# Sums of weight blocks made ahead on VectorE and kept in DRAM, and a first tile split on VectorE with first rows from ScalarE's queue

## The chip, the core and the metric

The kernel runs on one core of a Trainium2 chip. Its engines are TensorE (PE in the profile, its weight loads PEld), VectorE (DVE), ScalarE (ACT), GpSimd (POOL) and SyncE (SP). SyncE here only issues transfers; ScalarE and GpSimd issue a few as well. Each engine works through its own instructions in order and waits for others by semaphores. The metric is the device time of one execution in microseconds (us), lower is better. What a profile calls the span is the time from the first to the last instruction that it records.

## The reference

One encoder layer: a sandwich of RMSNorms around a gated neighbourhood attention, with 512 tokens (a grid of 8 x 64), width 2048, and 16 heads of 128, all in float32.

```python
h = rms_norm(x, norm_pre[i])
o, z = na_mixer(h, na_w_in[j], na_rpb[j])   # q, k, v, z = split(h @ w_in, 4); attention over 8 x 16 neighbours with a bias
y = (o * jax.nn.silu(z)) @ w_out
x = x + rms_norm(y, norm_post[i])
```

Nearly all of the work is the two products `h @ w_in` (512 x 2048 by 2048 x 8192) and `(...) @ w_out` (512 x 2048 by 2048 x 2048).

## The kernel before

**Numbers.** A float32 value is split into a high part `hi` (rounded to the matmul's fp32r form, a cast) and a low part `lo` (the value minus `hi`, a subtraction on VectorE). A product is then three matmuls: hi by hi, hi by lo, lo by hi. So each 128 x 512 block of weights W costs one cast (L247, ScalarE) and one subtraction (L248, VectorE) before it can be used. This is `prep(m)`; `m` counts the slots of the whole program, and `prep` runs two slots ahead (`AHEAD`) of the matmuls. Three `hi`/`lo` buffers go round.

**Steps.** The products are made in ten steps. Steps 0 and 8 are plain: 32 slots of 12 matmuls each. Steps 1 to 7 (the steady steps) and step 9 (`LAST`) use Strassen-Winograd: the four blocks B11, B12, B21, B22 of W are combined into seven operands, and seven passes of 8 slots with 6 matmuls each take the place of eight. Step 9 takes the passes in the order of `LATE`, 0, 1, 3, 4, 6, 5, 2. The sums of W that a pass needs are made in eight tiles `T[k]`, one for each block of rows k: pass 0 uses B11, pass 1 adds B12, pass 3 adds B22, pass 4 adds B21; pass 6 is B12 + B22 in the last step. Each addition is one VectorE instruction (L240) with a second operand `raw`, loaded from W into one of four buffers (`NRAW`). A raw load is issued by SP when its buffer is free and at least six preparations ahead. The other passes use one block alone, as `raw`.

**Beside the matmuls.** The attention of the heads (transposes, scores, exponentials, normalization) is laid between the slots by a table, `HEAD`, with calls `at(slot, function)`. In the last step the results are finished: `finish` squares and scales, `final` scales with the row's factor, adds x and writes out. The combining operations of the seven passes (`combine`, L359 to L380) are additions on VectorE that read the accumulators.

**Order.** Each engine's instructions are laid out by a scheduler that starts from the program's order and moves what is ready; what goes through `sync`, `dve` and `act` (the class `InOrder`) keeps its place in program order. Gated outputs of the heads are kept in DRAM by GpSimd's queue (`keep_g`, the tensor `graw`) and fetched for step 8.

**The start.** SP loads x0, raw0, x1, raw1, x2, raw2, x3 in turn, the first at 0.74 us and then one each 0.46 us or so. ScalarE issues the load of `gcol`, loads its activation table, multiplies x0 by `gcol` (`take_x`, L158), casts its two halves (`split_a`, L147) and then casts raw0 (L247). Transfers of one queue reuse eight semaphores, so a transfer can wait for the one eight places before it.

## Time and profile before

| what | us |
|---|---|
| median of 3 runs | 895.92 (895.0 to 896.43) |
| the profiled execution | 896.13 |
| its span | 894.4 |
| first plain matmul starts | 5.97 |
| steady steps, step 1 to step 7 | about 92 to 706 |
| last step's first matmul | 802.74 |
| last matmul starts | 883.83 |
| last instruction on VectorE ends | 890.1 |

The page gives, for each engine, its busy time; a table of windows gives the same for stretches of time. "Releaser" or "waits" name what an idle engine waited for. In a group of instructions `t<-t,raw` means: the tile t written from t and raw; buffer numbers are left out.

### The profile page before, as it was taken

To read this page: it belongs to the slowest core of one execution; us is meant where nothing else is said; L and a number is where in the kernel's file an instruction comes from. 1 tells how busy PE (TensorE), PEld (TensorE's weight loads), DVE (VectorE), ACT (ScalarE), POOL (GpSimd) and SP (SyncE) were. 2 spreads that over 40 slices of the span, in tenths; PEclk is the share of its full clock that TensorE was granted. 3 is DMA by queue.
4 is the path that set the end of the run, shared out by engine and by line. 5 is a ranking of instruction groups with operands and counts; after the bars stand their busy time and mean duration, and the time that the engine had idled before them with its cause. 6 is when DMAs were issued, how large, how long until landed. Compare 5 with 4: busy or idle time off the path is not lost. (4 is left out here: it accounts for less than half of the span.)

```text
span 894.4 us, 13143 instructions
## 1 busy us (share of the span) xinstructions
PE 877.7 (98%) x4184; PEld 729.3 (82%) x4184; DVE 733.8 (82%) x1367; ACT 560.7 (63%) x1093; POOL 21.0 (2%) x42
## 2 busy tenths in 40 slices
PE   9999999999999999999999999999999999999995
PEld 8888888888888888888888888888888788888774
DVE  4567979897988898889878987998799845979987
ACT  7666857585758565856675667566766755555451
POOL 0000000000000000000000000000010100000000
PEclk9999999999999999999999999999999999999998
DMA  8768357646763765377547654774486534447877
GB/s 267 210 178 257 97 173 237 204 121 184 234 192 109 223 216 178 115 224 226 167 121 226 210 174 124 235 211 149 147 271 218 157 100 139 141 141 226 269 231 239
DMA packets 88277, 168.65 MB, mean 189 GB/s; under 512 B 10128, under 2 KB 10128, under 8 KB 88208
## 3 DMA queue, kind: packets, MB, share of 16 engines
q1 hardware_dynamic: 85536, 159.95, 59.4%
q0 software_dynamic: 2240, 7.34, 2.4%
q8 instruction: 32, 0.52, 0.2%
q10 hardware_dynamic: 432, 0.53, 0.2%
q14 instruction: 37, 0.30, 0.1%
HBM read 159.92 MB, written 7.86 MB: 188 GB/s over the span
## 5 line engine op out<-in xcount | busy, mean ns | idle before, releaser
L247 ACT CAST hi<-t 128x512 fp32r<-128x512 f32 x320 | 196.6, 618 | 132.2 <-DVE lo L248 21.5
L248 DVE TENSOR_TENSOR lo<-t,hi 128x512 fp32r<-128x512 f32 x320 | 217.3, 686 | 33.5 <-ACT hi L247 32.7
L248 DVE TENSOR_TENSOR lo<-raw,hi 128x512 fp32r<-128x512 f32 x184 | 125.9, 688 | 68.6 <-ACT hi L247 46.9
L247 ACT CAST hi<-raw 128x512 fp32r<-128x512 f32 x184 | 113.8, 620 | 99.2 <-PE u L285 24.7
L240 DVE TENSOR_TENSOR t<-t,raw 128x512 f32<-128x512 f32 x200 | 134.0, 686 | 7.5 <-DMA raw<-in_w 6.6
L285 PE MATMUL u<-hi,a 128*128 128x512 f32 x512 | 130.9, 392 | 1.4 <-DVE e L380 1.2
L285 PEld LDWEIGHTS u<-hi,a 128*128 128x128 f32 x512 | 94.9, 188 | 21.5 <-DVE e L380 1.8
L285 PE MATMUL u<-lo,a 128*128 128x512 f32 x256 | 70.8, 389 | 0.0
L285 PEld LDWEIGHTS u<-lo,a 128*128 128x128 f32 x256 | 48.0, 188 | 10.0
L255 DVE TENSOR_TENSOR t<-t,raw 128x512 f32<-128x512 f32 x56 | 37.3, 686 | 7.3 <-DMA raw<-in_w 7.3
L332 PE MATMUL u9Y<-hi,a 128*128 128x512 f32 x96 | 26.6, 393 | 0.5 <-ACT hi L247 0.5
L332 PE MATMUL u1Y<-hi,a 128*128 128x512 f32 x96 | 26.8, 396 | 0.0
L332 PE MATMUL u2Y<-hi,a 128*128 128x512 f32 x96 | 26.8, 396 | 0.0
L332 PE MATMUL u4Y<-hi,a 128*128 128x512 f32 x96 | 26.8, 396 | 0.0
L332 PE MATMUL u3Y<-hi,a 128*128 128x512 f32 x96 | 26.8, 396 | 0.0
L332 PE MATMUL u5Y<-hi,a 128*128 128x512 f32 x96 | 26.8, 396 | 0.0
L332 PE MATMUL u7Y<-hi,a 128*128 128x512 f32 x96 | 26.8, 396 | 0.0
L332 PE MATMUL u6Y<-hi,a 128*128 128x512 f32 x96 | 26.8, 396 | 0.0
L332 PEld LDWEIGHTS u9Y<-hi,a 128*128 128x128 f32 x96 | 17.8, 188 | 5.4 <-ACT hi L247 1.4
L545 POOL DMA_DIRECT2D graw<-zm x14 | 7.8, 554 | 561.7 <-DVE zm L539 561.7
L495 ACT ACTIVATE edge<-edge,nm 128x192 f32<-128x192 f32 x32 | 14.5, 455 | 8.7 <-DVE nm L488 8.7
L332 PEld LDWEIGHTS u4Y<-hi,a 128*128 128x128 f32 x96 | 17.4, 188 | 3.2
(446 smaller groups left out, 1924.1 us busy)
## 6 DMA issues: line engine op xcount, KB each, us to landing
raw<-in_w SPq DMA_DIRECT2D x392, 256.0 KB, 3.0
t<-in_w SPq DMA_DIRECT2D x128, 256.0 KB, 3.0
bm<-in_rpb SPq DMA_DIRECT2D x16, 384.0 KB, 3.3
x<-in_xT SPq DMA_DIRECT2D x16, 256.0 KB, 3.9
graw<-zm POOLq DMA_DIRECT2D x14, 256.0 KB, 3.4
sq<-in_x SPq DMA_DIRECT2D x6, 512.0 KB, 6.2
xres<-in_x SPq DMA_DIRECT2D x12, 256.0 KB, 4.1
out<-xres SPq DMA_DIRECT2D x10, 256.0 KB, 3.0
```

What stands on the lines that cost most here:

```text
L240: nc.vector.tensor_tensor(T[k], T[k], src, ALU.add)
L247: nc.scalar.copy(hi, src)
L248: nc.vector.tensor_tensor(lo, src, hi.bitcast(F32), ALU.subtract)
L255: nc.vector.tensor_tensor(T[k], T[k], src, ALU.add)
L285: nc.tensor.matmul(U[n][j], l, r, start=k == 0 and i == 0, stop=k == KT - 1 and i == 2)
L332: nc.tensor.matmul(U[c][s], l, r, start=p in (0, 1, 4) and k == 0 and n == 0, stop=k == KH - 1 and n == 2, skip_group_check=True,)
L495: nc.scalar.activation(p, p, AF.Exp, bias=nm[:, i : i + 1], accum_out=sm[:, i : i + 1])
L545: nc.gpsimd.dma_start(graw[h], z_of[h])
```

## The change

**Sums of W for the last step.** The four sums that step 9 needs for each k (for passes 6, 1, 3 and 4) are made ahead, in steps 0 to 7. For each k, B12 and B22 of step 9 are loaded into two tiles Z (by SP for k = 0, by GpSimd's queue for the others). Four additions on VectorE follow, with B11 and B21 as `raw` loads that take their turn in the four raw buffers. Each sum is written to a DRAM tensor `wsum` by SP. The slots are in a list: four in each steady step, at slots 3, 16, 23 and 51 of the step. The Z tiles of the next k can be loaded only when the sums in them have been written out.

In step 9 the tile `T[k]` is loaded with the finished sum of the next pass as soon as its present content has been split; the additions and their raw loads are gone, and only the last pass (2) uses raw loads.

**The start.** raw0 and raw1 are loaded by ScalarE's queue. The activation table is loaded after that. The cast of raw0 is made on VectorE. For the first four k, ScalarE's multiplication and casts keep program order.

**Small tiles.** The four row-sum columns (`rc`, `rcy`, `ms`, `msy`) are slices of one tile `rows`, those of the softmax (`mx`, `sm`, `nm`, `rs`) of one tile `col`; `ms3` is `ms`.

```diff
-    nc.scalar.preload_act_table_set("exp_and_others")
...
+    Z = [cp.tile([P, L], F32, name=f"z{i}") for i in range(2)]
+    wsum = dp.tile([NPASS, KH, P, L], F32, name="wsum")
+    LATE_W = {p: wsum[p] for p in (1, 3, 4, 6)} | {0: w[LAST, B11], 5: w[LAST, B22]}
+
+    SUMS = ((1, None, 6), (0, B11, 1), (1, B11, 3), (1, B21, 4))
+
+    def load_z(k):
+        for t, q in zip(Z, (B12, B22)):
+            (nc.gpsimd if k else nc.sync).dma_start(t, w[LAST, q, k])
+
+    def sum_z(k, i):
+        z, add, p = SUMS[i]
+        if i in (1, 3):
+            sum_z.raw = raws.pop(N + 2 * k + i // 2)
+        nc.vector.tensor_tensor(Z[z], Z[z], Z[0] if add is None else sum_z.raw, ALU.add)
+
+    def keep_z(k, i):
+        z, _, p = SUMS[i]
+        nc.sync.dma_start(wsum[p, k], Z[z])
...
     def take_x(k):
-        nc.scalar.activation(X[k], X[k], AF.Copy, scale=gcol[:, k : k + 1])
-        take(k)
+        scalar = act if k < 4 else nc.scalar
+        scalar.activation(X[k], X[k], AF.Copy, scale=gcol[:, k : k + 1])
+        take(k, scalar)
...
+    slots = [base(step) + c for step in range(1, NSTEP) for c in (3, 16, 23, 51)]
+    sums = {}
+    for k in range(KH):
+        for i in range(4):
+            sums.setdefault(slots[3 * k + k // 2 + (0, 1, 1, 2)[i]], []).append((k, i))
+    first = {k: slots[3 * k + k // 2 - 1] + 3 if k else base(1) - 8 for k in range(KH)}
...
     def load_raw(m):
         raws[m] = wp.tile([P, L], F32, tag="raw", name=f"raw{m}", bufs=NRAW)
+        if m >= N:
+            k, i = divmod(m - N, 2)
+            nc.sync.dma_start(raws[m], w[LAST, (B11, B21)[i], k])
+            return
...
-        nc.sync.dma_start(raws[m], src)
+        (nc.scalar if m < 2 else nc.sync).dma_start(raws[m], src)
...
-        if not plain and (p in (1, 3, 4) or step == LAST and p == 6):
+        if step < NSTEP and not plain and p in (1, 3, 4):
             nc.vector.tensor_tensor(T[k], T[k], src, ALU.add)
...
-        nc.scalar.copy(hi, src)
+        if m == 0:
+
+            nc.vector.tensor_copy(hi, src)
+        else:
+            (act if m < 4 else nc.scalar).copy(hi, src)
         nc.vector.tensor_tensor(lo, src, hi.bitcast(F32), ALU.subtract)
-        if plain:
+        if step == LAST:
+            i = LATE.index(p)
+            if i + 2 < NPASS:
+                nc.sync.dma_start(T[k], LATE_W[LATE[i + 1]][k])
+        elif plain:
...
+    for k in range(KH):
+        at(first[k], load_z, k)
...
+    nc.scalar.preload_act_table_set("exp_and_others")
     for m in range(-AHEAD, N):
         if m + AHEAD < N - KH:
             prep(m + AHEAD)
+            for j in z_raws(m + AHEAD):
+                for r in at_prep.get(j, ()):
+                    load_raw(r)
+            for k, i in sums.get(m + AHEAD, ()):
+                sum_z(k, i)
+                at(m + AHEAD + 1, keep_z, k, i)
```

The change in the order is shown at three places. The first is VectorE at the very start: `raw_156` and `raw_154` are the first tile of W, `a_0` and `a_1` the two halves of a block of x. Before:

```order
L148 TENSOR_TENSOR a_0_110<-x_154,a_0_110 128x256 [waits Activation_49]
L148 TENSOR_TENSOR a_1_111<-x_154,a_1_111 128x256 [waits Activation_49]
L248 TENSOR_TENSOR lo_174<-raw_156,hi_173 128x512 [waits DMAHW2_49,Activation_49]
L248 TENSOR_TENSOR lo_187<-raw_160,hi_186 128x512 [waits DMAHW4_49,Activation_49]
L148 TENSOR_TENSOR a_0_114<-x_158,a_0_114 128x256 [waits Activation_49]
```

and now:

```order
L286 CAST hi_172<-raw_154 128x512 [waits DMAHW2_49]
L289 TENSOR_TENSOR lo_173<-raw_154,hi_172 128x512 [waits DVE_49]
L169 TENSOR_TENSOR a_0_108<-x_152,a_0_108 128x256 [waits Activation_49]
L169 TENSOR_TENSOR a_1_109<-x_152,a_1_109 128x256 [waits Activation_49]
L169 TENSOR_TENSOR a_0_112<-x_156,a_0_112 128x256 [waits Activation_49]
```

The cast of the first tile now stands on VectorE and waits for its load alone; both parts of W stand ahead of the two low parts of x.

The second place is VectorE at the turn from step 3 to step 4, where the fourth row block's last sum and the fifth one's first sum stand (`z_149` and `z_148` are the two Z tiles; DMASW is GpSimd's queue). In the run of splits L248 of the profile, these rows now stand:

```order
L289 TENSOR_TENSOR lo_3691<-t_142,hi_3690 128x512 [waits Activation_49]
L141 TENSOR_TENSOR z_149<-z_149,raw_3744 128x512 [waits DMAHW5_49,DMAHW0_49,DVE_49]
L289 TENSOR_TENSOR lo_3704<-t_143,hi_3703 128x512 [waits PE_49,Activation_49]
L443 TENSOR_TENSOR vl_0_3753<-s_3_2988,vh_0_3752 128x512 [waits Activation_49]
L289 TENSOR_TENSOR lo_3718<-t_144,hi_3717 128x512 [waits DVE_49,PE_49,Activation_49]
L289 TENSOR_TENSOR lo_3729<-t_145,hi_3728 128x512 [waits PE_49,Activation_49]
L289 TENSOR_TENSOR lo_3740<-t_146,hi_3739 128x512 [waits PE_49,Activation_49]
L289 TENSOR_TENSOR lo_3759<-t_147,hi_3758 128x512 [waits PE_49,Activation_49]
L289 TENSOR_TENSOR lo_3770<-t_140,hi_3769 128x512 [waits DMAHW4_49,PE_49,Activation_49]
L141 TENSOR_TENSOR z_149<-z_149,z_148 128x512 [waits DMASW5_49,DMASW3_49]
L277 TENSOR_TENSOR t_140<-t_140,raw_3813 128x512 [waits DMAHW1_49,DVE_49]
L289 TENSOR_TENSOR lo_3780<-t_141,hi_3779 128x512 [waits DMAHW6_49,PE_49,Activation_49]
```

The scheduler has moved the first sum of the fifth block up to eight rows behind the last sum of the fourth, both in the same tile `z_149`. In between, the fourth block's sum has to be written out and the fifth block's B22 loaded. In the profile of before the first and the last but three of these rows are the splits at 344.25 and 352.00 us.

The third place is VectorE in the last step, ahead of the combining operations of pass 4 (L363 before, L408 now), which TensorE waits for before it goes on with pass 6. `a_2` is the low part of a block of the final pass, prepared early. Before:

```order
L240 TENSOR_TENSOR t_144<-t_144,raw_8849 128x512 [waits DMAHW4_49,DMAHW0_49]
L248 TENSOR_TENSOR lo_8845<-t_149,hi_8844 128x512 [waits PE_49,Activation_49]
L240 TENSOR_TENSOR t_145<-t_145,raw_8864 128x512 [waits DMAHW7_49,DMAHW5_49]
L248 TENSOR_TENSOR lo_8861<-t_142,hi_8860 128x512 [waits PE_49,Activation_49]
L248 TENSOR_TENSOR a_2_116<-raw_8877,a_3_117 128x512 [waits DMAHW1_49,Activation_49]
L248 TENSOR_TENSOR lo_8874<-t_143,hi_8873 128x512 [waits PE_49,Activation_49]
L363 TENSOR_TENSOR e_8765<-u9Z_8777,e_8765 128x512 [waits PE_49]
```

and now:

```order
L289 TENSOR_TENSOR a_2_122<-raw_8918,a_3_123 128x512
L289 TENSOR_TENSOR lo_8856<-t_147,hi_8855 128x512 [waits DMAHW1_49,PE_49,Activation_49]
L289 TENSOR_TENSOR lo_8871<-t_140,hi_8870 128x512 [waits DMAHW2_49,PE_49,Activation_49]
L289 TENSOR_TENSOR a_2_126<-raw_8944,a_3_127 128x512 [waits DMAHW2_49,Activation_49]
L289 TENSOR_TENSOR lo_8882<-t_141,hi_8881 128x512 [waits DMAHW4_49,PE_49,Activation_49]
L408 TENSOR_TENSOR e_8790<-u9Z_8799,e_8790 128x512 [waits PE_49]
```

The additions are gone, and the low parts of the final pass stand further up: this is the fifth of eight, where it was the second before.

## The prediction

> **What bounds the kernel now.** I read the page's busy times first, then a table by stage, then who TensorE waited for.

> ```profile
> PE 877.7 (98%) x4184; PEld 729.3 (82%) x4184; DVE 733.8 (82%) x1367; ACT 560.7 (63%) x1093; POOL 21.0 (2%) x42
> ...
> 0.00:6.00 6.00, 4.75 (x25) 4.56 (x25) 0.98 (x4) 3.32 (x6) 0.91 (x9) 1.00 0.67 207
> 6.00:90.00 84.00, 84.00 (x371) 69.55 (x372) 52.84 (x101) 55.89 (x106) 1.57 (x1) 1.00 0.78 228
> 90.00:700.00 610.00, 609.09 (x2970) 509.04 (x2969) 529.48 (x981) 403.17 (x784) 13.22 (x24) 1.00 0.60 185
> 700.00:720.00 20.00, 18.84 (x94) 15.32 (x93) 16.27 (x39) 15.07 (x34) 1.09 (x2) 1.00 0.43 122
> ...
> 802.70:835.50 32.80, 32.80 (x145) 26.83 (x144) 30.96 (x51) 17.83 (x32) 0.00 (x0) 1.00 0.75 224
> 835.50:860.20 24.70, 23.27 (x101) 18.62 (x100) 20.27 (x32) 11.30 (x20) 0.00 (x0) 1.00 0.84 257
> 860.20:884.10 23.90, 22.14 (x93) 16.76 (x91) 21.90 (x45) 10.63 (x25) 2.63 (x3) 1.00 0.79 247
> 884.10:894.40 10.30, 0.12 (x1) 0.00 (x0) 5.34 (x9) 0.69 (x2) 0.54 (x1) 0.73 0.68 215
> ```

> The columns are the stretch, its length, the busy time of TensorE's matmuls, its weight loads, VectorE, ScalarE and GpSimd, the granted clock, the share of the DMA engines and GB/s. TensorE is the bound: it is busy 98% at a granted clock of 1.00, and in the seven steady steps (inside 90 to 700) it idles 0.9 of 610 us. Time can only be won where it isn't running: the first 6 us, the last step (802.7 to 884.1) and the 10.3 us behind the last matmul. VectorE is the one to watch: 529 of 610 us in the steady steps, 30.96 of 32.8 us in the first three passes of the last step.

> ```profile
> PE u9Z L332 <- DVE e L363: 1.4, 1, 1.4
> PE u9Y L332 <- DVE lo L248: 1.3, 2, 1.0
> PE u L285 <- DVE e L380: 1.2, 1, 1.2
> ...
> PE u9Y L332 <- ACT hi L247: 0.5, 1, 0.5
> ```

> These are TensorE's longest waits after the start. All but the 1.2 us (at 705 us, before the plain step) lie in the last step, on tiles named u9. How much that step loses in all follows from the chain of waits, which merges matmuls of one tile, and from the last matmul in the timeline:

> ```profile
> 802.74 10.88 PE u9X L332 x48
> 813.62 22.05 PE u9Y L332 x96
> ...
> 883.83 0.39 PE L332 MATMUL u9X<-a 128*128 128x512 f32 x1
> ```

> 48 matmuls in 10.88 us are 0.227 us each. The last step has 7 x 48 = 336, or 76.2 us. From 802.74 to 883.83 + 0.23 it took 81.3 us: **5.1 us are lost**, of which the waits above are 3.2 and slow restarts and small gaps the rest.

> **The last step.** The change takes 32 additions (passes 1, 3, 4 and 6, eight each) from VectorE there, and replaces 56 loads of W by 48 after pass 0. Why TensorE stood still at 847 us is seen on VectorE:

> ```profile
> 845.47 0.69 DVE L248 TENSOR_TENSOR lo<-t,hi 128x512 fp32r<-128x512 f32 x1
> 847.12 0.69 DVE L248 TENSOR_TENSOR a<-raw,a 128x512 fp32r<-128x512 f32 x1 [0.96 <-ACT a L247]
> ...
> 848.33 1.28 DVE L363 TENSOR_TENSOR e<-u9Z,e 128x512 f32<-128x512 f32 x2
> ...
> 849.07 1.33 PE L332 MATMUL u9Z<-hi,a 128*128 128x512 f32 x4 [1.43 <-DVE e L363]
> ```

> The accumulator that pass 6 goes on with is read by L363, and L363 stands behind preparations that wait for a raw load. That load was late because the four raw buffers were held by operands of the additions. Afterwards the same loads go to the eight T tiles as soon as the preceding pass has split a tile, so each has eight slots, 8 x 1.36 = 10.9 us, less the some 3 us by which preparation runs ahead. A load lands in

> ```profile
> raw<-in_w SPq DMA_DIRECT2D x392, 256.0 KB, 3.0
> ...
> graw<-zm POOLq DMA_DIRECT2D x14, 256.0 KB, 3.4
> ```

> 3.0 us (median; the columns are count, size and us to landing). Four of the eight raw loads of the final pass also move ahead of the step, into the raw buffers that are now free. What could be late next is VectorE at the change from pass 6 to pass 5, where four combining operations stand before the split of the third tile. They end some 2.4 us after the pass, the split 0.6 later, and TensorE wants its result after two slots and four matmuls, 3.6 us: 0.6 us to spare. I leave 0.5 us of loss in the step and take **-4.6 us**; the bounds are 0 (a new wait of the same length) and -5.1.

> **Behind the last matmul.**

> ```profile
> 885.23 0.75 DVE L668 SCALAR_TENSOR_TENSOR t<-s,rcy,t 128x512 f32<-128x512 f32 x1
> 885.89 0.69 DVE L656 TENSOR_TENSOR c<-u9X,gpost 128x512 f32<-128x512 f32 x1
> ```

> The last accumulator is ready at about 884.3, but VectorE takes it at 885.89, since it is still finishing the rows before. In the new order seven matmuls of the last pass that stood among those of pass 5 stand behind them, so pass 5 ends with 44 still to come instead of 37: 7 x 0.227 = 1.6 us more in which VectorE can finish, and one split fewer stands there. The 1.6 us of delay go almost wholly: **-1.2 us**, between 0 and -1.6.

> **The steady steps** get the 32 additions, 16 loads by GpSimd's queue (two of the 16 by SP's), 16 raw loads and 32 writes by SP's. An addition costs VectorE

> ```profile
> L240 DVE TENSOR_TENSOR t<-t,raw 128x512 f32<-128x512 f32 x200 | 134.0, 686 | 7.5 <-DMA raw<-in_w 6.6
> ```

> 0.69 us, and 0.60 from start to start in a dense run (353.97, 354.57 below). That is 32 x 0.60 = 19.2 us in stretches where 529 of 610 are taken: VectorE goes to 90%. What hides it is that VectorE waits for ScalarE there. The place with the least cover, by the order shown above, is the fourth row block's sum, between the split at 352.00 and the addition behind it:

> ```profile
> 344.25 0.69 DVE L248 TENSOR_TENSOR lo<-t,hi 128x512 fp32r<-128x512 f32 x1
> ...
> 352.00 0.69 DVE L248 TENSOR_TENSOR lo<-t,hi 128x512 fp32r<-128x512 f32 x1 [0.67 <-ACT hi L247]
> 352.72 0.69 DVE L240 TENSOR_TENSOR t<-t,raw 128x512 f32<-128x512 f32 x1
> 353.36 0.69 DVE L248 TENSOR_TENSOR lo<-t,hi 128x512 fp32r<-128x512 f32 x1
> 353.97 0.68 DVE L379 TENSOR_TENSOR s<-u3Z,s 128x512 f32<-128x512 f32 x1
> 354.57 0.68 DVE L380 TENSOR_TENSOR e<-e,u3Z 128x512 f32<-128x512 f32 x1
> ```

> The splitting row waits 0.67 us for ScalarE, as its neighbours do, so VectorE has that much to spare in a slot of 1.36 us. But this sum waits for a load that GpSimd can issue only once the preceding sum has been written out. The preceding sum follows the split at 344.25 and ends near 345.5; with 0.4 us to issue the write, 3.4 to land (the graw row, also a write to DRAM), 0.55 to issue the load and 3.4 to land it comes in at about 353.3, while VectorE is there at 352.7. So it stands 0.6 us and adds 0.6, and behind it the combining operations leave no gap. Two of the six such places (the fourth and fifth block) are like this; the other four lie among splits that wait 0.67 us each. Also queued behind the waiting sum are splits, and TensorE behind these; behind a waiting write on SP's queue are raw loads, which SP mostly holds until VectorE frees a buffer anyway. I take **+0.6 us**: half of the 1.2 us at two places, the rest under the slots that VectorE is ahead. The bounds are 0 and all 19.2. The first block's first sum falls into the first plain step, where VectorE has 52.84 of 84 us and TensorE never idles: nothing. The small columns that now share a tile cost nothing either: by the order, the same instructions wait for the same engines as before.

> **The start.** On ScalarE and TensorE:

> ```profile
> 3.93 0.72 ACT L158 ACTIVATE x<-x,gcol 128x512 f32<-128x512 f32 x1 [1.46 <-DMA gcol<-in_gpre]
> 4.68 0.71 ACT L147 CAST a<-x 128x256 fp32r<-128x256 f32 x2
> 5.30 0.61 ACT L247 CAST hi<-raw 128x512 fp32r<-128x512 f32 x1
> ...
> 5.97 2.11 PE L285 MATMUL u<-hi,a 128*128 128x512 f32 x8 [0.20 <-ACT hi L247]
> ...
> L139 SPq DMA_DIRECT2D x<-in_xT x6: 388/428/432, 0.7 to 11.0; - x6
> ...
> DMA to landing us min/median/max: 3.0/3.5/5.5
> ...
> L229 SPq DMA_DIRECT2D raw<-in_w x7: 327/416/432, 1.2 to 10.6; - x7
> ...
> DMA to landing us min/median/max: 3.2/3.2/4.1
> ```

> The last four lines are the issues of the first x and raw loads (count, ns to issue, first and last start) and their times to landing. The first cast of W stands third on ScalarE and ends at 5.91. On VectorE it needs only the load, issued at 1.2 as now: 1.2 + 3.2 = 4.4 us. No single-input cast on VectorE is in the trace; its bounds are 0 and the 0.69 of its two-input form, and I take 0.69: 5.1 us. The first part of x (4.68 + 0.36) is ready at 5.04. TensorE starts at 5.2 instead of 5.97, and VectorE's four operations before the second x part end 0.1 or 0.2 late: **-0.6 us**, between 0 and -1.0. [...] The table load, now behind two issues of 0.4 us, still ends before 3.9.

> Sum: -4.6 - 1.2 + 0.6 - 0.6 = -5.8 us from the profiled execution's 896.13, or 890.3. The median shown is 0.2 lower than that execution: **890.1 us**.

> **Rivals.**

> 1. *The sums show through* (slower). If VectorE's lead is gone wherever a sum stands, each costs its 0.6 us, and the six loads by GpSimd's queue another 1.0 each: 25 us at most. Half of that, 12.6, against gains of 6.4 gives 902. For it speaks VectorE's load in some stretches:

> ```profile
> 220.00:240.00 20.00, 20.00 (x101) 16.68 (x100) 19.91 (x43) 14.16 (x31) 0.54 (x1) 1.00 0.70 213
> ```

> It is busy 19.91 of 20 us here. Against it speaks that the sums stand mostly where rows wait 0.67 us for ScalarE. It decides from 6.4 us on: 0.2 us for each sum. Chance 9%.
> 2. *The wait turns into one for DMA.* The last step's DMA share is 0.75 to 0.84. If the T loads come late as the raw loads did, the step keeps its 5.1 us and only start and tail remain: 895. Against it are the eight loads fewer and the 8 us of lead. Chance 8%.
> 3. *ScalarE's queue brings nothing.* Two transfers that run at once share the engines, so x's first rows, issued at 0.7 and landed 3.0 us later, at 3.7, may land with W's at 4.4; then ScalarE starts 0.5 us later and the start gains 0.1: 890.6 us. [...] Chance 35%, of which nothing leaves the forecast's own range.

> **How the numbers follow.** The forecast's case (with or without rival 3) has 75%, between 888 and 893; a steady loss of 2 to 5 us has another 8%, up to 894.5. The range is 887.8 to 894.0. About 0.2%, 1.8 us, is what a measurement of this kernel can tell from no change: faster than 894.1 in 82%, within 0.2% in 9% (rival 2 and the worst steady loss), slower 9%.

> **What would show it.** Right: TensorE's waits on u9 gone or below 0.5 us in all, 336 matmuls in under 77 us; the first L285-form matmul near 5.2; a write, then a GpSimd load, then a short VectorE wait at six sums. Wrong: new TensorE waits on lo or hi inside the steady steps of more than 2 us, or last-step casts that wait for t<-wsum.

## The result: slower, with the profile after

| what | before | after |
|---|---|---|
| median, us (runs of the same chip) | 895.48 (4 runs) | 909.05 (4 runs) |
| ratio, 95% interval | | 1.0152 (1.0126 to 1.0178) |
| profiled execution / its span | 896.13 / 894.4 | 911.46 / 909.4 |
| first plain matmul starts | 5.97 | 5.81 |
| from there to the last step's first matmul | 796.6 | 816.4 |
| last step, first to last matmul start | 81.3 | 77.2 |
| last matmul start to the end of the span | 10.5 | 10.0 |

The forecast was 890.1, between 887.8 and 894.0. The start, the last step and the tail all became shorter, by 0.2, 4.1 and 0.5 us. The 20 us in between turned the sum round. By step, from its first matmul to that of the next one, in us (s1 is step 1; s7 ends at the second plain step):

| kernel | s1 | s2 | s3 | s4 | s5 | s6 | s7 |
|---|---|---|---|---|---|---|---|
| before | 87.5 | 87.0 | 86.8 | 87.2 | 87.7 | 86.8 | 87.1 |
| after | 88.6 | 87.8 | 87.0 | 90.6 | 97.1 | 89.8 | 88.9 |

From the page of the kernel after: busy times, one of the costliest groups (busy time, mean ns of one, idle time just before it and what ended it), and transfers with their median us to landing.

```profile
PE 885.1 (97%) x4184; PEld 730.4 (80%) x4184; DVE 730.1 (80%) x1368; ACT 559.8 (62%) x1092; POOL 28.8 (3%) x56
...
L141 DVE TENSOR_TENSOR z<-z,z 128x512 f32<-128x512 f32 x8 | 5.5, 690 | 19.3 <-DMA z<-in_w 19.3
...
raw<-in_w SPq DMA_DIRECT2D x366, 256.0 KB, 3.0
t<-in_w SPq DMA_DIRECT2D x128, 256.0 KB, 4.0
wsum<-z SPq DMA_DIRECT2D x32, 256.0 KB, 3.6
...
z<-in_w POOLq DMA_DIRECT2D x14, 256.0 KB, 4.2
```

The second line is the finding: VectorE stood 19.3 us in front of the eight first sums of a row block, for the load of their tile. VectorE is no busier than before (730 against 734 us); it waits. Who TensorE waited for, in all, how often, and the longest:

```profile
PE u5X L377 <- DVE lo L289: 3.1, 2, 2.4
PE u4X L377 <- DVE lo L289: 2.8, 2, 1.5
...
PE u5Z L377 <- DVE lo L289: 1.1, 1, 1.1
PE u6Z L377 <- DVE lo L289: 0.9, 1, 0.9
```

These are the new waits on `lo` in the steady steps, named beforehand as what would show the forecast wrong. They aren't the whole loss: over steps 1 to 7 TensorE is idle 11.8 us in place of 0.9, and the same matmuls keep it busy for 617.9 us in place of 609.1. Some 3 of these 8.8 us are a lower clock (last section); the rest was not traced to single places. VectorE's timeline at the worst place, the turn from step 4 to step 5 (start, length, instruction; in brackets the idle time before it and what ended it), then SP's and GpSimd's issues there, then TensorE:

```profile
441.23 2.67 DVE L289 TENSOR_TENSOR lo<-t,hi 128x512 fp32r<-128x512 f32 x4
444.56 0.69 DVE L289 TENSOR_TENSOR lo<-t,hi 128x512 fp32r<-128x512 f32 x1 [0.67 <-ACT hi L288]
449.72 0.69 DVE L141 TENSOR_TENSOR z<-z,z 128x512 f32<-128x512 f32 x1 [4.46 <-DMA z<-in_w]
...
453.92 1.28 DVE L289 TENSOR_TENSOR lo<-t,hi 128x512 fp32r<-128x512 f32 x2
```

```profile
441.12 0.42 SPq L145 DMA_DIRECT2D wsum<-z  x1
...
446.74 0.54 POOL L135 DMA_DIRECT2D z<-in_w  x1 [7.81 <-DMA wsum<-z]
```

```profile
448.24 1.07 PE L377 MATMUL u5X<-hi,a 128*128 128x512 f32 x4
451.67 0.73 PE L377 MATMUL u5X<-lo,a 128*128 128x512 f32 x2 [2.35 <-DVE lo L289]
452.24 1.66 PE L377 MATMUL u5X<-hi,a 128*128 128x512 f32 x4
454.66 1.22 PE L377 MATMUL u5X<-lo,a 128*128 128x512 f32 x2 [0.77 <-DVE lo L289]
```

Read in order: the finished sum is written out from 441.12, GpSimd may issue the next load only at 446.74, VectorE stands until 449.72, the splits queued behind the sum are late, and TensorE stops twice.

### The profile page after: what moved, and what is told of

Read it like the earlier page. It is cut to its first block, busy times and chain, and to the rows that moved or that the text cites. A ratio compares the mean times of both kernels' runs of the same rounds, so it can differ in the third digit from the quotient of the medians.

```text
span 909.4 us, 13192 instructions
## 1 busy us (share of the span) xinstructions
PE 885.1 (97%) x4184; PEld 730.4 (80%) x4184; DVE 730.1 (80%) x1368; ACT 559.8 (62%) x1092; POOL 28.8 (3%) x56
## 5 line engine op out<-in xcount | busy, mean ns | idle before, releaser
L288 ACT CAST hi<-t 128x512 fp32r<-128x512 f32 x328 | 201.5, 619 | 133.1 <-DVE lo L289 24.1
L289 DVE TENSOR_TENSOR lo<-t,hi 128x512 fp32r<-128x512 f32 x328 | 221.5, 684 | 35.9 <-ACT hi L288 31.3
L289 DVE TENSOR_TENSOR lo<-raw,hi 128x512 fp32r<-128x512 f32 x176 | 120.2, 687 | 66.7 <-ACT hi L288 40.5
L288 ACT CAST hi<-raw 128x512 fp32r<-128x512 f32 x172 | 106.7, 621 | 103.8 <-PE u L330 29.1
L277 DVE TENSOR_TENSOR t<-t,raw 128x512 f32<-128x512 f32 x168 | 112.1, 683 | 9.1 <-DMA raw<-in_w 8.7
L300 DVE TENSOR_TENSOR t<-t,raw 128x512 f32<-128x512 f32 x56 | 37.5, 682 | 3.6 <-DMA raw<-in_w 3.5
L432 ACT ACTIVATE s<-s,rows 128x512 f32<-128x512 f32 x28 | 19.4, 716 | 12.8 <-DVE s L424 9.8
L141 DVE TENSOR_TENSOR z<-z,z 128x512 f32<-128x512 f32 x8 | 5.5, 690 | 19.3 <-DMA z<-in_w 19.3
L377 PEld LDWEIGHTS u5Y<-hi,a 128*128 128x128 f32 x96 | 17.4, 188 | 4.3 <-ACT hi L288 1.0
## 6 DMA issues: line engine op xcount, KB each, us to landing
raw<-in_w SPq DMA_DIRECT2D x366, 256.0 KB, 3.0
t<-in_w SPq DMA_DIRECT2D x128, 256.0 KB, 4.0
wsum<-z SPq DMA_DIRECT2D x32, 256.0 KB, 3.6
t<-wsum SPq DMA_DIRECT2D x32, 256.0 KB, 3.2
x<-in_xT SPq DMA_DIRECT2D x16, 256.0 KB, 4.8
z<-in_w POOLq DMA_DIRECT2D x14, 256.0 KB, 4.2
graw<-zm POOLq DMA_DIRECT2D x14, 256.0 KB, 4.0
```

The lines of the kernel that those rows point to most:

```text
L141: nc.vector.tensor_tensor(Z[z], Z[z], Z[0] if add is None else sum_z.raw, ALU.add)
L277: nc.vector.tensor_tensor(T[k], T[k], src, ALU.add)
L288: (act if m < 4 else nc.scalar).copy(hi, src)
L289: nc.vector.tensor_tensor(lo, src, hi.bitcast(F32), ALU.subtract)
L300: nc.vector.tensor_tensor(T[k], T[k], src, ALU.add)
L377: nc.tensor.matmul(U[c][s], l, r, start=p in (0, 1, 4) and k == 0 and n == 0, stop=k == KH - 1 and n == 2, skip_group_check=True,)
```

## Experiments

Each ran beside the kernel before on the same chip; ratios are to it, with the 95% interval. "Above no_sums" in the text compares ratios, in us of 895.5.

**pin_first_sum.** Only the order on VectorE is changed.

```diff
-        nc.vector.tensor_tensor(Z[z], Z[z], Z[0] if add is None else sum_z.raw, ALU.add)
+        (nc.vector if i else dve).tensor_tensor(Z[z], Z[z], Z[0] if add is None else sum_z.raw, ALU.add)
```

> The changed kernel with the first sum of each row block (B12 + B22) kept in program order; work, loads and writes are the same. Before it stood 5 to 9 rows behind the preceding block's last sum, now 15 to 80 rows. Theory 1 (VectorE stands at this sum, 19.3 us in all, while the Z tile is written out and loaded anew, and the splits queued behind it make TensorE wait): the waits on z<-in_w go below 1 us, the steady steps lose at most 2 us against before, and the gains stay (last step 4.0, tail 0.6, start 0.2 us): about 891 us, not above 893. Theory 2 (32 additions x 0.60 = 19.2 us of VectorE's time show through): about 909 us as the change. Theory 3 (80 more transfers delay the loads of W): 905 to 909 us.

900.48 us, ratio 1.0068 (1.0054 to 1.0082). About 7.5 us of the loss are gone by order alone, and no first sum waits for its load any more. It isn't all: a second wait of the same kind became visible, in the timeline of VectorE and then TensorE:

```profile
347.02 0.68 DVE L289 TENSOR_TENSOR lo<-t,hi 128x512 fp32r<-128x512 f32 x1
351.02 0.69 DVE L141 TENSOR_TENSOR z<-z,raw 128x512 f32<-128x512 f32 x1 [3.33 <-DMA wsum<-z]
```

```profile
352.37 0.74 PE L377 MATMUL u3Z<-lo,a 128*128 128x512 f32 x2 [2.57 <-DVE lo L289]
```

The fourth sum overwrites the tile of the third, which is still being written out. It stood like this twice, 3.33 and 1.88 us.

**z_loaded_once.** The place of the first sum stays, its load goes.

```diff
-    for k in range(KH):
-        at(first[k], load_z, k)
+    at(first[0], load_z, 0)
```

> The changed kernel without the Z loads of row blocks 1 to 7 (left out: the fresh B12 and B22, so the last step works on sums of other values); all 32 sums, 16 raw loads and 32 writes stay, and the first sum of a block still stands 5 rows behind the last one, waiting for its write alone. Theory 1: the 19.3 us of waiting fall to under 5, about 891 to 895 us. Theory 2: about 909. Theory 3: 14 of 80 transfers are gone, about 905.

897.02 us, ratio 1.0023 (1.0012 to 1.0033). Together with pin_first_sum: against before, taking away the place ahead of the landing removes over half of the loss, taking away the load most of it. Here 14 transfers are gone as well, and the first sums still stand 9.7 us in all for the write, with the kernel only some 6 us above no_sums:

```profile
L141 DVE TENSOR_TENSOR z<-z,z 128x512 f32<-128x512 f32 x8 | 5.5, 691 | 10.0 <-DMA wsum<-z 9.7 <-DMA z<-in_w 0.3
```

So a microsecond of standing is no fixed price. Both runs miss theory 1 in size, so something else costs too.

**no_sums.** The gain without the price.

```diff
-    LATE_W = {p: wsum[p] for p in (1, 3, 4, 6)} | {0: w[LAST, B11], 5: w[LAST, B22]}
+    LATE_W = {p: w[LAST, q] for p, q in ((0, B11), (1, B12), (3, B22), (4, B21), (6, B12), (5, B22))}
...
-            sums.setdefault(slots[3 * k + k // 2 + (0, 1, 1, 2)[i]], []).append((k, i))
+            pass
...
-    for k in range(KH):
-        at(first[k], load_z, k)
```

> The changed kernel with nothing of the sums in the steady steps: no Z loads, additions, raw loads for them or writes; the last step loads its T tiles from single blocks of W (left out: all sums of the last step). All theories: start, last step and tail as in the change, steady steps as before: 895.5 - 4.8 = 890.7 us. What pin_first_sum takes above this is the cost of the sums without the wait.

890.59 us, ratio 0.9954 (0.9941 to 0.9967), as expected. The change loses 1.98% from here: 17.7 us.

**transfers_only.** Meant to show the transfers by themselves.

```diff
-        if i in (1, 3):
-            sum_z.raw = raws.pop(N + 2 * k + i // 2)
-        nc.vector.tensor_tensor(Z[z], Z[z], Z[0] if add is None else sum_z.raw, ALU.add)
...
-        return [N + 2 * k + i // 2 for k, i in sums.get(m, ()) if i in (1, 3)]
+        return []
```

> The changed kernel with the 16 Z loads and the 32 writes, but without the 32 additions and their 16 raw loads (left out: the sums; the writes hold plain blocks). VectorE never touches a Z tile, so it can't wait for one. Theory 1: as no_sums, about 891. Theory 2: as no_sums, about 891. Theory 3 (transfers crowd each other): 48 of 64 to 80 transfers are there, some 902 us.

909.61 us, ratio 1.0169 (1.0155 to 1.0184), but for a reason of its own: with no addition to wait for, the scheduler moved the writes and loads forward, the first at 32.96 us, and they ran bunched in the first plain step and step 1. All the loss is there; steps 2 to 6 took 86.9 us each. It says nothing on spread transfers.

**pin_all_sums.** All four sums keep program order.

```diff
-        nc.vector.tensor_tensor(Z[z], Z[z], Z[0] if add is None else sum_z.raw, ALU.add)
+        dve.tensor_tensor(Z[z], Z[z], Z[0] if add is None else sum_z.raw, ALU.add)
```

> As pin_first_sum, but all four sums of a row block keep program order: the last sum stands 9 to 90 rows behind the one whose tile is being written out, not 5, so the 3.3 us wait for wsum<-z that stopped TensorE 2.9 us at 349 us is gone. Theory 1 (only standing for Z transfers, either way, costs): 892 us, the 9.9 us above no_sums are nearly gone. Theory 2 (the additions' own time shows where VectorE has no gap, in slots 3 and 23 of a step): 900.5 less about 3.5 = 897 us. Theory 3 (transfers): also 897, with waits on raw or t loads.

896.44 us, ratio 1.0014 (1.0002 to 1.0026). The second wait is gone, with about 5 us; the first sums wait 0.6 us in all:

```profile
L64 DVE TENSOR_TENSOR z<-z,z 128x512 f32<-128x512 f32 x8 | 5.5, 686 | 0.6 <-DMA z<-in_w 0.6
```

What is left above no_sums, 0.60% or 5.4 us, is no wait for a Z tile.

**vector_only.** VectorE's share of that.

```diff
+        dve.tensor_tensor(Z[z], Z[z], Z[0] if add is None else sum_z.raw, ALU.add)
...
-    for k in range(KH):
-        at(first[k], load_z, k)
+    at(first[0], load_z, 0)
...
-                at(m + AHEAD + 1, keep_z, k, i)
```

(`LATE_W` as in no_sums.)

> As pin_all_sums, but without the writes of the sums and with one pair of Z loads only; the last step loads its T tiles from single blocks of W (left out: the sums never reach the last step). VectorE's 32 additions and their 16 raw loads stay. Theory 1: 891 us as no_sums. Theory 2: as pin_all_sums, about 897. Theory 3: 891.

893.53 us, ratio 0.9975 (0.9966 to 0.9985): 0.21%, some 1.9 us above no_sums for 32 additions and 16 raw loads. The sums' own time is nearly hidden; theory 2 is out as the main cause.

**transfers_spread.** As transfers_only, with writes that keep their place.

```diff
-        nc.sync.dma_start(wsum[p, k], Z[z])
+        sync.dma_start(wsum[p, k], Z[z])
```

> As transfers_only (16 Z loads, 32 writes, no additions and none of their raw loads; left out: the sums), but the writes keep program order on SyncE, so they spread over steps 1 to 7 instead of filling steps 0 and 1. Theories 1 and 2: 891 us as no_sums. Theory 3: 896 us or more, with the loss in steps 1 to 7.

899.39 us, ratio 1.0050 (1.0033 to 1.0067), 0.96% or 8.6 us above no_sums with no addition at all. Theory 3 holds after all, as a second cause: spread transfers cost, too. Since this kernel also fixed the order of the writes on SP, its size isn't that of the change.

**placed_sums** and **placed_same_slot** put the sums where VectorE seemed to have room: in the kernel before it is busy only 58 or 59% of the time while TensorE is at slots 10 to 17 of steps 2 to 7. All sums keep program order, as in pin_all_sums. The code of the first, without that line; the second has 18, 18 for 16, 18 and 20, 20 for 18, 20:

```diff
-    slots = [base(step) + c for step in range(1, NSTEP) for c in (3, 16, 23, 51)]
+    slots = {k: [base(k) + c for c in ((12, 16, 18, 51) if k else (14, 18, 20, 26))] for k in range(KH)}
...
-            sums.setdefault(slots[3 * k + k // 2 + (0, 1, 1, 2)[i]], []).append((k, i))
+            sums.setdefault(slots[k][i], []).append((k, i))
-    first = {k: slots[3 * k + k // 2 - 1] + 3 if k else base(1) - 8 for k in range(KH)}
+    first = {k: slots[k - 1][3] + 3 if k else 6 for k in range(KH)}
```

> As pin_all_sums, with other places: row block 0 in the first plain step, one block in each of steps 1 to 7, at slots 12, 16, 18 and 51, where VectorE has 14 to 30 per cent free before the change, and at least 5 slots between a sum and the one that must wait for its write or its load. All work and transfers are there. Theory 1: as pin_all_sums (892). Theory 2: 891 to 892, about 5 us under pin_all_sums, since the additions fall into gaps. Theory 3: as pin_all_sums.

> As placed_sums, but the second and the third sum of a row block, which share one raw operand, stand in the same slot (12, 18, 18, 51), as they do in the change, so that this operand holds one of the four raw buffers for one slot, not three. Ring theory (the held buffer delays the loads behind it, VectorE stands for raw loads at the additions of pass 3 and the k and q rows come late): the 13.9 us of VectorE's waits on raw there fall to under 8, and the time comes to pin_all_sums or below, 894 to 897 us. Place theory (the transfers of the sums crowd the raw loads of pass 3 wherever they stand in slots 12 to 18): about 905 us as placed_sums.

907.61 us, ratio 1.0138 (1.0118 to 1.0158), and 908.27, ratio 1.0127 (1.0107 to 1.0147). The expected gain of placed_sums missed by some 16 us, and of the theories for placed_same_slot that of the place came out: no sum waits, and yet every steady step is 0.9 to 2.8 us longer than in no_sums. In placed_same_slot VectorE's waits on raw in `t<-t,raw` (L277) fell from 13.9 to 7.4 us and the time didn't move, so the ring theory is out.

**placed_vector_only** takes the writes and the reloads out of placed_same_slot, by the edits of vector_only.

> As placed_same_slot, without the writes of the sums and with one pair of Z loads only; the last step loads single blocks of W (left out: the sums never reach the last step). Additions and their raw loads at slots 12, 18, 18 and 51 stay. If VectorE's own time at these slots makes the 12 to 17 us (each step's k rows come 1.0 to 1.3 us late): about 905 us, as placed_same_slot. If the transfers do (writes and Z loads crowd the raw loads of pass 3): 891 to 894, as vector_only.

893.38 us, ratio 0.9973 (0.9960 to 0.9986): as vector_only. The additions cost the same little even there; the writes and Z loads make the other 1.54%, 13.8 us. Over the whole kernel, ScalarE's casts waited longer for raw loads, first with these transfers and then without:

```profile
ACT hi L288 <- DMA raw<-in_w: 30.6, 26, 2.1
```

```profile
ACT hi L287 <- DMA raw<-in_w: 19.3, 18, 1.6
```

Slots 18 to 24 and 24 to 30 of step 4, in the table by stage, in the same order:

```profile
388.30:398.80 10.50, 10.50 (x57) 8.89 (x56) 7.09 (x12) 4.46 (x9) 0.55 (x1) 1.00 0.92 288
398.80:410.80 12.00, 10.86 (x57) 8.72 (x56) 12.00 (x21) 8.13 (x15) 0.54 (x1) 1.00 0.78 246
```

```profile
383.10:393.60 10.50, 10.50 (x57) 8.89 (x56) 9.20 (x16) 5.31 (x9) 0.00 (x0) 1.00 0.82 259
393.60:404.20 10.60, 10.59 (x56) 8.72 (x55) 9.83 (x18) 7.28 (x14) 0.54 (x1) 1.00 0.77 225
```

The columns are as in the prediction. With the transfers the DMA engines are at 0.92, and VectorE gets 7.09 us done in place of 9.20. It makes this up in the next stretch at 12.00 of 12 us, too late: TensorE idles 1.1 us there. That late raw loads are the way from the transfers to this loss fits these rows, but no run shows it by itself. VectorE's idle time at slots 10 to 17 wasn't itself a wait for DMA: in the kernel before, 24.3 of its 25.8 us there (steps 2 to 7) were ended by ScalarE's casts. The additions found room in it; their transfers didn't, in the slots behind.

**only_sum6** and **late_t_only** look for a part worth keeping. The first is shown in part: its one addition also keeps program order, and `LATE_W` and the raw loads of the last step are fitted to the one sum. The second is an edit of the kernel before.

```diff
+    sums = {base(k) + (51 if k else 26): [(k, 0)] for k in range(KH)}
+    first = {k: base(k) + (4 if k else 10) for k in range(KH)}
...
-        if step < NSTEP and not plain and p in (1, 3, 4):
+        if not plain and p in (1, 3, 4):
...
-            if i + 2 < NPASS:
+            if p in (4, 6):
```

> The start of the change, and of the sums only the first one (for pass 6): 8 additions, 16 Z loads and 8 writes, one block in each step, addition pinned at slot 51 (block 0 in the first plain step). The last step makes the sums of passes 1, 3 and 4 as before, loads its T tiles with the finished sum for pass 6 and with plain B22 for pass 5; nothing is left out. If the gain in the last step came from the raw buffers and VectorE's additions around pass 6, most of the 4 us comes with a quarter of the additions and no wait for a Z tile: steady cost 0.7 (a quarter of 2.9) + about 1, gain 3 to 4.8, so 892 to 894 us. If the gain needs all four sums: 896.

```diff
-        return step in PLAIN or p not in (0, 6) or step == LAST and p == 6
+        return step in PLAIN or p not in ((0, 5) if step == LAST else (0, 6))
...
+        elif step == LAST and p == 6:
+            nc.sync.dma_start(T[k], w[LAST, B22, k])
```

> The kernel before with one edit, no sums at all: in the last step pass 5 takes its operand (B22) from the T tile, loaded as soon as pass 6 has split it, instead of from a raw buffer; the number of loads is the same. If the gain of the last step came mostly from raw buffers being free at passes 6 and 5: 1 to 3 us faster, 892 to 894. If it came from the additions taken away: 895, as before.

896.47 us, ratio 1.0003 (0.9992 to 1.0013), and 895.39, ratio 0.9991 (0.9980 to 1.0002): neither can be told from before. In late_t_only the last step was 1.5 us shorter, and the stretch behind it 1.2 us longer, in one profile. In only_sum6 the last step gains 0.8 us, not 4, and the wait at the change from pass 4 to pass 6 is longer than the 1.4 before:

```profile
PE u9Z L372 <- DVE e L403: 2.3, 1, 2.3
```

Behind this wait the granted clock was half for 3.4 us, which cost an estimated 1.7 us more (half of 3.4); the two make 4.0 of the 4.4 us that this step loses there against 336 x 0.227. So raw buffers freed around pass 6 don't remove the wait at that change; the longest wait of the last step fell below 1 us (0.3 to 0.8) in the runs in which all additions were gone from it.

**turn_sums** tries the places that cost pin_all_sums least.

```diff
+    slots = {k: [base(k) + c for c in ((51, 59, 59, 72) if k else (14, 20, 20, 26))] for k in range(KH)}
```

(The rest as in placed_sums.)

> All sums, loads and writes as in pin_all_sums, all additions pinned, with the pattern that cost pin_all_sums least (0.3 to 0.5 us in its steps 2 and 3) used for every row block: first sum at slot 51, second and third at slot 3 of the next step, fourth at its slot 16; block 0 stands in the first plain step, the end of block 7 in the second plain step. If the places of pin_all_sums in step 5 (second and third sum at slot 23, 3.0 us over no_sums there) made much of its 5.8 us: 890.6 + 7 x 0.4 = 893 to 894 us, faster than before. If any place costs its 0.7 us for each sum: 896 as pin_all_sums.

895.81 us, ratio 0.9998 (0.9988 to 1.0007). The best full version: it gives back all of the loss and wins nothing. Its profiled execution was its fastest of 11, 893.54, so the 893 of the first expectation does occur, but the runs reach 897.75. No version that computes everything was measurably faster than before.

## Why the prediction was wrong

**The step that failed** is the term of the steady steps, +0.6 us: "So it stands 0.6 us and adds 0.6", with two such places. The mechanism was the one described, a sum that waits for a write and a load; its size and the number of places without cover were wrong. The very place that was worked out, VectorE after the fourth block's last sum, reads after:

```profile
348.30 0.69 DVE L141 TENSOR_TENSOR z<-z,raw 128x512 f32<-128x512 f32 x1 [0.75 <-DMA wsum<-z]
...
354.00 0.69 DVE L289 TENSOR_TENSOR lo<-t,hi 128x512 fp32r<-128x512 f32 x1 [0.67 <-ACT hi L288]
358.29 0.69 DVE L141 TENSOR_TENSOR z<-z,z 128x512 f32<-128x512 f32 x1 [3.60 <-DMA z<-in_w]
```

```profile
349.01 0.33 SPq L266 DMA_DIRECT2D raw<-in_w  x1
349.74 0.33 SPq L124 DMA_DIRECT2D t<-in_w  x1
350.11 0.44 SPq L145 DMA_DIRECT2D wsum<-z  x1
```

```profile
355.39 0.54 POOL L135 DMA_DIRECT2D z<-in_w  x1 [7.05 <-DMA wsum<-z]
```

From the end of the sum (348.99) to the landing of the next load are 9.3 us where the sum said 7.8: SP issued the write 1.1 us after the sum, not at once, behind a raw and a T load; from its issue 5.3 us passed until GpSimd issued, against 0.4 + 3.4; the load landed 2.9 us later, against 0.55 + 3.4. VectorE arrived after 5.7 us instead of 7.2. Twice 1.5 us more: 3.6 instead of 0.6. A difference of two estimates of 7 us, taken as known to half a microsecond, was the weak point.

- *Two of the six such places; the others lie among splits that wait 0.67 us each.* All six sums waited, 2.0 to 4.5 us, 3.2 on average, where 0.6 was taken; the first block's waited 0.3. The two waits of some 2 us, in steps 2 and 3, were nearly covered: these steps are 0.8 and 0.2 us longer than before. Steps 4 to 6, with the four of 3.3 to 4.5 us, are 3.0 to 9.4 us longer.
- *The transfers* were priced at nothing beyond the wait. That is where the rest went: transfers and additions together cost 5.4 us with nearly every wait for a Z tile gone (pin_all_sums), and by vector_only about 1.9 of that are the additions.
- *The wait of the fourth sum for the write of the third* was not seen at all: 1.5 us on VectorE in the change and 5.2 in pin_first_sum, which stayed 4.8 us above pin_all_sums.

So the 17.7 us above no_sums fall, by runs, into about 1.9 for the additions, 3.5 for transfers, 4.8 for the fourth sum's place and 7.5 for the first one's, each by a difference of ratios good to some 1 to 2 us. The order in which they are taken away matters, so these are not separate prices. Why the transfers cost what they do is open: transfers_spread, without any addition, lost more (8.6 us), in another order of SP's queue.

**Rival 1**, the slower one (902 us, 9%), had the sign and the ground, VectorE's in-order queue, but named the sums' own time, which costs 1.9 us. **Rival 2** fell: the wait at L408, a combining operation, is 0.5 us, as left in the sum.

```profile
PE u9Z L377 <- DVE e L408: 0.5, 1, 0.5
```

**The last step** was right: -4.6 forecast, -4.1 measured, in the chain of waits and the last matmul of the timeline:

```profile
822.41 10.88 PE u9X L377 x48
...
899.40 0.39 PE L377 MATMUL u9X<-a 128*128 128x512 f32 x1
```

**Behind the last matmul** -1.2 was forecast and -0.5 came. VectorE takes the last accumulator 1.2 us after the last matmul's start instead of 2.1, but it now waits for ScalarE just before:

```profile
900.61 0.69 DVE L700 TENSOR_TENSOR c<-u9X,gpost 128x512 f32<-128x512 f32 x1 [1.13 <-ACT ysq L699]
```

**The start** was over-sized: -0.6 against -0.2, near rival 3's 0.1 in size. Rival 3's late ScalarE didn't come: ScalarE took the first x at 3.75 us, against 3.93 before. It was W's load that came late. On ScalarE's queue, on VectorE and on TensorE:

```profile
1.19 0.93 ACTq L266 DMA_DIRECT2D raw<-in_w  x2
```

```profile
5.08 0.43 DVE L286 CAST hi<-raw 128x512 fp32r<-128x512 f32 x1 [4.08 <-DMA raw<-in_w]
```

```profile
5.81 2.09 PE L330 MATMUL u<-hi,a 128*128 128x512 f32 x8
```

From the load's issue to the cast are 3.9 us, not the 3.2 taken, and from the cast's end to the first matmul 0.3, not 0.1; that ate most of what the new place of the cast won. The cast took 0.43 us, less than the 0.69 taken. In the profiles of the other kernels with this start the first matmul began between 5.46 and 6.20, so 0.2 us is no measured gain. From ScalarE's queue W's load came no sooner after its issue (3.9 us) than from SP's (3.2). What rival 3 says of transfers that run at once shows in x's loads of the first 12 us: issued among W's, at a DMA share of 0.9 and more between 2.5 and 8.5 us, they took 3.0 us to land at least and 5.5 at most; in the kernel after, 2.8 and 5.7.

## What to carry to other kernels

A sum that refills its own buffer through DRAM puts a write, an issue and a load in front of an in-order engine: count the whole round trip (9.3 us here) from the instruction that frees the buffer, and look up in the final order, not in the source, how many instructions lie in between. Such a wait costs whoever is queued behind it, so the engine's own extra work (1.9 us) says little. And room on one engine isn't room for the transfers that the added work brings: placed in VectorE's gaps, the additions cost some 1.7 us and their writes and reloads 13.8.

## What was not expected of the hardware

```profile
448.00:452.50 4.50, 2.15 (x10) 1.45 (x9) 2.78 (x5) 0.25 (x1) 0.00 (x0) 1.00 0.42 137
452.50:456.00 3.50, 2.73 (x7) 1.72 (x6) 3.44 (x7) 3.50 (x7) 0.00 (x0) 0.51 0.14 54
456.00:459.50 3.50, 3.50 (x12) 2.78 (x12) 2.45 (x4) 1.67 (x4) 0.00 (x0) 0.52 0.29 78
459.50:463.00 3.50, 3.50 (x21) 2.95 (x20) 3.03 (x5) 2.26 (x4) 0.00 (x0) 1.00 0.19 35
```

TensorE was busy 6.1 us of the 6.8 at half clock, 3.0 more than at full clock. Some 0.7 of these fall before the second wait, which would otherwise have been that much longer; so an estimated 2.3 us are lost to the clock alone. The same shows after the 2.57 us wait in pin_first_sum:

```profile
352.50:356.00 3.50, 3.50 (x11) 2.72 (x11) 2.77 (x5) 1.15 (x2) 0.00 (x0) 0.62 0.86 266
```

The length of a wait alone doesn't order the cases. A wait of 1.78 us in placed_same_slot (until 719.66) was followed by half clock; one of 1.77 in placed_sums (until 719.61) and one of 2.33 in transfers_only (until 112.93) were not. In the profiles of before and after the changes of the clock lie multiples of one length apart: after, it rises at 5.39 us, falls at 452.54, rises at 459.36 and falls at 903.10, with 447.15, 6.83 and 443.73 us between, which are 131, 2 and 130 times 3.413; before, 884.05 us lie between the rise at 4.79 and the fall at 888.84, 259 times as much. In stretches of this length, counted from the first rise, the kernel after had TensorE idle for 2.35 us in the one that ends with the fall at 452.54, and for 1.49 at most in any other up to the last matmul; before, where the clock held all that time, it was 1.21 at most. In placed_same_slot the wait lies in one stretch, the first row, with 1.79 us idle; the 2.33 us of transfers_only are split over two, with 1.74 and 0.62 us idle:

```profile
716.84:720.25 3.41, 1.62 (x8) 1.04 (x7) 3.41 (x8) 3.40 (x8) 0.00 (x0) 1.00 0.70 180
720.25:723.66 3.41, 3.41 (x10) 2.65 (x9) 2.16 (x5) 1.98 (x5) 0.00 (x0) 0.50 0.38 127
```

```profile
108.90:112.31 3.41, 1.67 (x6) 1.05 (x6) 2.17 (x4) 3.38 (x7) 0.55 (x1) 1.00 0.88 272
112.31:115.73 3.42, 2.80 (x12) 2.31 (x13) 3.34 (x6) 2.81 (x7) 0.55 (x1) 1.00 0.73 276
```

Of these rows, 1.79 us of idle time in one stretch were followed by half clock and 1.74 were not; what sets the clock is not shown. For placed_sums, idle 0.6 us from 714 to 718 and 1.6 from 718 to 722, it is not shown where the stretches begin. The idle times rest on modelled ends of matmuls, so the difference between 1.74 and 1.79 is no sharper than the model. The clock is part of why step 5 is the longest of all, 9.4 us over before; it also holds two of the long waits, 4.46 and 3.54 us.
